# Two edits in a two-block sequence kernel: the keys' norm stands with the queries' norm, and attention divides by its sums once per query block

## The chip, the cores and the metric

The kernel runs on one core of a Trainium2 chip. The metric is device time in microseconds (us), the median over runs; smaller is better. Engines are named as in the profile: PE is TensorE's matmul, PEld its weight load, DVE is VectorE, ACT is ScalarE, POOL is GpSimd, SP is SyncE. L984 means line 984 of the kernel before. In the changed kernel the code from L805 on stands ten lines lower or so (its L853, L864, L869, L923 and L931 are the L843, L854, L859, L913 and L921 of before); this text uses the numbers of before, and only rows that are quoted from the changed kernel carry its own.

## The reference

Input and output are 1024 tokens of 1024 features. The first block has two layers of convolution beside sparse attention, and only its attention matters here; a second block (gated recurrences and an MLP) follows.

```python
def dsa_attention(c_q, c_kv, k_idx, w_idx, q_norm_g, w_uq, w_qidx, kv_norm_g, w_uv, rel_bias):
    k_top = 256
    cq = rmsnorm(c_q, q_norm_g)                          # [1, 1024, 256]
    q = (cq @ w_uq)                                      # 8 heads of 128
    q_idx = (cq @ w_qidx)                                # 8 index heads of 64
    kv = rmsnorm(c_kv, kv_norm_g)                        # [1, 1024, 128], one for all heads
    ...
    score = einsum("bth,bths->bts", w, relu(q_idx . k_idx))   # causal
    _, sel = top_k(score, k_top)                         # 256 keys of each query
    logits = q . kv[sel] * 128 ** -0.5 + rel_bias
    o = softmax(logits) . kv[sel]
    return einsum("bshc,hcd->bshd", o, w_uv)             # 8 heads of 64

x = x + gate * rmsnorm(concat(y_conv, y_attn * silu(g_attn)) @ w_out)
```

## The kernel before

Products in full precision are made of three matmuls of split operands (hi and lo, `mm3`, L269 to L271; the splits are L264 on ACT and L265 on DVE). Activations of a layer lie transposed, features on partitions and the 1024 tokens in two halves of 512 columns. SBUF is cut into pages of 1024 words.

A layer goes through these stages, each of them a generator that yields after a unit of work:

- **Conv inputs**, then **latents** (`g_latents`): keys' latent `kv`, index keys, queries' latent `cq` and its norm. The norm of a half is: Square on ACT (L796), sum over partitions by matmuls with ones (L302), Ln and Exp on ACT (L294, L297, inverse square root), a multiplication on DVE (L801), a split. Ln and Exp need function tables (L288 loads the one that has both).
- **Index scores** (`g_scores`): blocks of 128 queries; c=0 are blocks 2 to 4, c=1 blocks 5 to 7. For each pair of index heads PE makes the heads' queries (copied by L843 on ACT, L844 on DVE) and the products with the index keys (L852); ACT copies these out of PSUM (L854), DVE adds them up (L857, L859).
- **Top-k** (`g_topk`): the 256th largest score of each query is found bit by bit, 31 bits. top1 has blocks 2 to 4: block 2 is counted on DVE (L921), blocks 3 and 4 on ACT (L913), and POOL makes the next threshold from ACT's count (L916, L917, L919). top2 has blocks 5 and 6 on DVE and 7 on ACT.
- **Keys**: `norm_keys` (L984) normalises `kv` by the same steps as the queries (its multiplication is L994), `split_keys` (L998) makes the keys' hi and lo and, by 8 matmuls (L1010), the heads' values.
- **Queries** of all heads, **attention** (`g_attn`, L1095): blocks 0 to 4 while top2 is still counting, then blocks 5 to 7 with the masks of top2. Then the output projection.

Work that fills gaps runs beside these: the convolution (`g_conv`, whose taps are the L703 on DVE) and the gates (`g_gates`, L269 to L271 and L689).

The order on each engine is fixed before the program starts, by a scheduler that works from the order in which the code emits instructions; each engine then runs its own instructions strictly in that order. `weave` interleaves generators in proportion to the units named for each, and `bg=[(generator, rate)]` advances a generator by that many steps for each such unit:

```python
weave((pr(g_latents(), 9), 6), bg=[(conv, RATES[l][1])])     # L1023, RATES[l][1] = 2.0
...
weave((pr(g_scores(wq, 0), 4), 24), (part(gates, g1), g1), bg=[(conv, RATES[l][2])])
weave((pr(g_scores(wq, 1), 4), 24), (part(gates, g2), g2), bg=[(top1, RATES[l][3]), (conv, RATES[l][10])])
norm_keys()
keys = split_keys()
weave((gates, g3_), (top1, 37), bg=[(conv, RATES[l][10]), (top2, RATES[l][5])])
```

In attention a pair of heads has its logits (L1116 to L1124), maximum (L1130 with a mask, L1134 to L1137 without), Exp with the row sum (L1138), and then 1 / sum (L1141), which two matmuls with the identity spread over 64 rows for each head (L1145), the gate's product with it (L1147), transposes (L1154, L1160), values (L1164), and the product of values and gate (L1168).

## Time and profile before

| | |
|---|---|
| median of 3 runs | 3030.16 us (3029.22 to 3030.83) |
| span of the profiled execution | 3029.3 us |
| its own time | within the three runs above, the span is 0.9 us below their median |
| PE | 2906.8 us busy, 96% of the span |
| DVE | 2229.9 us, 74% |
| ACT | 1679.8 us, 55% |
| POOL | 247.2 us, 8% |
| chain that ended last | PE 58%, DVE 5%, POOL 2%, ACT 2%, DMA 1% |
| L913 on ACT | 186 counts, 166.8 us busy, 36.1 us idle until POOL's L919 |

The whole span is PE at 96%, but the two stretches from the first index scores to the end of top2 are not: there DVE and ACT are as full as PE, and POOL, which does nothing elsewhere, is busy. These stretches (196 to 507 us in layer 0, 891 to 1187 us in layer 1) hold nearly everything that the change touches. In the rows below a duration followed by [x <-E t Ln] means that the engine sat idle for x us before it and that instruction Ln of engine E ended that.

### The profile page before, as it was taken

To read this page: it belongs to the slowest core of one execution; us is meant where nothing else is said; L and a number is where in the kernel's file an instruction comes from. 1 tells how busy PE (TensorE), PEld (TensorE's weight loads), DVE (VectorE), ACT (ScalarE), POOL (GpSimd) and SP (SyncE) were. 2 spreads that over 40 slices of the span, in tenths; PEclk is the share of its full clock that TensorE was granted. 3 is DMA by queue.
4 is the path that set the end of the run, shared out by engine and by line. 5 is a ranking of instruction groups with operands and counts; after the bars stand their busy time and mean duration, and the time that the engine had idled before them with its cause. 6 is when DMAs were issued, how large, how long until landed. Compare 5 with 4: busy or idle time off the path is not lost.

```text
span 3029.3 us, 40735 instructions
## 1 busy us (share of the span) xinstructions
PE 2906.8 (96%) x15235; PEld 2362.8 (78%) x15235; DVE 2229.9 (74%) x4118; ACT 1679.8 (55%) x3032; POOL 247.2 (8%) x630
## 2 busy tenths in 40 slices
PE   9998787999999888999999999999999999999999
PEld 6877565778877665777888888888888888888887
DVE  5998899776988899756555667656666587776875
ACT  6248766737147866646444466555555654454454
POOL 0005511000005511000000000000000000000000
PEclk9999989999999989999999999999999999999999
DMA  8222102154101200133122211101013344456443
GB/s 276 63 40 63 42 18 77 48 193 149 39 18 42 63 19 18 36 112 118 49 62 62 79 35 36 56 29 56 29 37 122 103 143 153 151 201 238 153 146 111
DMA packets 218637, 264.14 MB, mean 87 GB/s; under 512 B 11504, under 2 KB 153543, under 8 KB 218439
## 3 DMA queue, kind: packets, MB, share of 16 engines
q1 hardware_dynamic: 218438, 261.54, 26.7%
q8 instruction: 119, 1.95, 0.3%
q14 instruction: 80, 0.65, 0.1%
HBM read 201.21 MB, written 60.29 MB: 86 GB/s over the span
## 4 chain that ended last, share of the span: by engine, by line
PE 58%; DVE 5%; POOL 2%; ACT 2%; DMA 1%; issue 1%; POOLq 0%; ACTq 0%
PE ps L269 15%; PE ps L271 15%; PE ps L270 15%; PE ps L331 5%; PE ps L1499 2%; DVE pg L921 2%; POOL consts L917 1%; PE ps L1164 1%; PE ps L1154 1%; POOL consts L919 1%; POOL consts L916 1%; DMA pg<-in_w_in_dram 1%; PE ps L1488 0%; DVE pg L1130 0%; PE ps L498 0%
## 5 line engine op out<-in xcount | busy, mean ns | idle before, releaser
L269 PE MATMUL ps<-pg,pg 128*128 128x512 f32 (+2 forms) x3080 | 1178.7, 384 | 15.1 <-DVE pg L265 4.2
L270 PE MATMUL ps<-pg,pg 128*128 128x512 f32 (+2 forms) x3080 | 1176.3, 383 | 0.0
L271 PE MATMUL ps<-pg,pg 128*128 128x512 f32 (+2 forms) x3080 | 1176.0, 382 | 0.0
L264 ACT ACTIVATE pg<-pg 128x512 fp32r<-128x512 f32 (+2 forms) x884 | 481.7, 591 | 527.7 <-PE ps L271 157.2
L269 PEld LDWEIGHTS ps<-pg,pg 128*128 128x128 f32 x3080 | 580.5, 189 | 132.9 <-DVE pg L265 10.1
L271 PEld LDWEIGHTS ps<-pg,pg 128*128 128x128 f32 x3080 | 580.6, 189 | 109.8 <-issue 3.7
L270 PEld LDWEIGHTS ps<-pg,pg 128*128 128x128 f32 x3080 | 580.8, 189 | 107.9 <-issue 3.5
L265 DVE TENSOR_TENSOR pg<-pg,pg 128x512 fp32r<-128x512 f32 (+2 forms) x884 | 528.2, 636 | 136.4 <-ACT pg L264 121.3
L278 POOL TENSOR_TENSOR consts<-consts 128x1 f32<-128x1 f32 x56 | 31.3, 559 | 2069.0 <-DVE consts L277 2069.0
L913 ACT ACTIVATE pg<-pg,consts 128x512 bf16<-128x512 uint16 (+5 forms) x186 | 166.8, 897 | 40.8 <-POOL consts L919 36.1
L703 DVE SCALAR_TENSOR_TENSOR pg<-pg,consts,pg 128x512 f32<-128x512 f32 (+15 forms) x256 | 176.9, 742 | 0.4
L331 PE MATMUL ps<-pg,pg 128*128 128x512 f32 x768 | 175.9, 389 | 0.0
L921 DVE TENSOR_SCALAR_CACHE_REDUCE pg<-pg,consts 128x384 bf16<-128x384 uint16 (+5 forms) x186 | 170.9, 919 | 2.3
L331 PEld LDWEIGHTS ps<-pg,pg 128*128 128x128 f32 x768 | 143.8, 188 | 29.6
L1138 ACT ACTIVATE pg<-pg,consts 128x256 f32<-128x256 f32 (+7 forms) x128 | 98.9, 774 | 70.2 <-DVE consts L1130 51.7
L1154 PE MATMUL ps<-consts,pg 128*128 128x128 f32 x576 | 107.7, 291 | 1.9 <-ACT pg L1160 1.1
L852 PE MATMUL ps<-pg,pg 128*128 128x512 f32 (+3 forms) x320 | 86.3, 370 | 14.7 <-DVE pg L844 9.4
L1164 PE MATMUL ps<-pg,pg 128*64 128x128 f32 x1152 | 92.5, 292 | 5.8 <-DVE pg L1147 1.7
L1116 PE MATMUL ps<-pg,pg 128*128 128x384 f32 (+5 forms) x192 | 79.4, 415 | 16.2 <-DVE consts L1130 7.9
L1160 ACT ACTIVATE pg<-ps 128x512 f32<-128x512 f32 (+1 forms) x112 | 57.8, 532 | 66.8 <-PE ps L1154 62.4
L917 POOL TENSOR_SCALAR consts<-consts 128x1 f32<-128x1 f32 x186 | 78.0, 419 | 179.1 <-ACT pg L913 173.5
L1164 PEld LDWEIGHTS ps<-pg,pg 128*64 128x64 f32 x1152 | 64.1, 141 | 35.1 <-issue 13.4
(350 smaller groups left out, 3810.7 us busy)
## 6 DMA issues: line engine op xcount, KB each, us to landing
pg<-in_w_in_dram SPq DMA_DIRECT2D x104, 512.0 KB
pg<-hidden SPq DMA_DIRECT2D x56, 512.0 KB
hidden<-pg SPq DMA_DIRECT2D x48, 512.0 KB
pg<-in_w_ada_dram SPq DMA_DIRECT2D x32, 512.0 KB
pg<-in_w_up_dram SPq DMA_DIRECT2D x32, 512.0 KB
pg<-in_w_down_dram SPq DMA_DIRECT2D x32, 512.0 KB
pg<-in_w_out_dram SPq DMA_DIRECT2D x24, 512.0 KB
x<-pg SPq DMA_DIRECT2D x24, 512.0 KB
```

Source lines behind the costliest of these rows:

```text
L264: self.nc.scalar.activation(hi, src, AF.Copy)
L265: self.nc.vector.tensor_sub(lo, src, hi.bitcast(F32))
L269: nc.tensor.matmul(ps, lhsT=wl, rhs=rh, start=first, stop=False)
L270: nc.tensor.matmul(ps, lhsT=wh, rhs=rl, start=False, stop=False)
L271: nc.tensor.matmul(ps, lhsT=wh, rhs=rh, start=False, stop=last)
L331: nc.tensor.matmul(ps, lhsT=w[z][k], rhs=act[y][k][:, a:b], start=k + n == 0, stop=3 * k + n == 3 * kt - 1)
L703: nc.vector.scalar_tensor_tensor(out, x[:, :512 - d], w, prev[:, d:], op0=OP.mult, op1=OP.add)
L913: nc.scalar.activation(junk_a(b), keys[b], AF.Sign, scale=-1.0, bias=col(tk["half"], b), accum_out=col(tk["cnt"], b))
L917: nc.gpsimd.tensor_scalar(col(tk["tm"], b), col(tk["cnt"], b), lim, -step, op0=OP.is_gt, op1=OP.mult)
L921: nc.vector.tensor_scalar(junk_d(b), keys[b], col(tk["cand"], b), None, op0=OP.is_ge, op1=OP.add, accum_out=col(tk["cnt"], b))
L1154: nc.tensor.transpose(pt[:, c:c + 128], Ps[hi][:, j * 128:j * 128 + 128], self.ident)
L1164: nc.tensor.matmul(uv[hi * 64:hi * 64 + 64], lhsT=V[j // 2][:, v:v + 64], rhs=th[:, jj * 256 + hi * 128:jj * 256 + hi * 128 + 128], start= ...
```

## The change

- `norm_keys` is gone. Its steps stand at the end of `g_latents`, behind the queries' norm, on the same scratch page and function table, in the rotation of PSUM banks 4 to 7 instead of bank 3. `g_latents` has so a seventh unit, and the weave count goes from 6 to 7, so that `conv` (rate 2.0) is advanced by two more steps there.
- In `g_attn` the sums of all eight heads of a query block go to one tile of 8 columns. With the last pair of heads there is one reciprocal of 128x8, eight matmuls that spread it (as many as before in all), one product of the gate of 128x512 and, at the end of the block, one product of values and gate of 128x512. The values of the four pairs lie side by side in PSUM bank 6.
- Two tiles of 8 columns take the place of four of 2; comments and docstrings are gone.

```diff
@@ g_latents
                     self.split(cqh[j][:, s], cql[j][:, s], cq[j][:, s])
                 yield
+            for s in halves:
+                sq = t[:, s]
+                nc.scalar.activation(sq, kv[:, s], AF.Square)
+                ps = self.bank("t", s4)
+                self.sum_rows(ps, [sq])
+                self.bcast_rstd(sq, ps, 128, tab)
+                nc.vector.scalar_tensor_tensor(kv[:, s], kv[:, s], self.vec[f"kv_norm_g{l}"][:, 0:1], sq, op0=OP.mult,
+                                               op1=OP.mult)
+            yield
             self.free(t, cq)
-        def norm_keys():
-            kv = lat["kv"]
-            t = self.page()
-            tab = self.ln_table()
-            for s in halves:
...
-        weave((pr(g_latents(), 9), 6), bg=[(conv, RATES[l][1])])
+        weave((pr(g_latents(), 9), 7), bg=[(conv, RATES[l][1])])
-        norm_keys()
@@ g_attn
+                sm = self.ring("sums", self.sums)
+                uvs = self.bank("pu", [6])
                 for hp in range(4):
...
-                    nc.vector.reciprocal(sm, sm)
-                    pu = self.bank("pu", [6])
-                    uv, rb = pu[:, :128], pu[:, 128:256]
-                    for hi in range(2):
-                        nc.tensor.matmul(rb[hi * 64:hi * 64 + 64], lhsT=sm[:, hi:hi + 1].to_broadcast([128, 64]),
-                                         rhs=self.ident, start=True, stop=True)
-                    nc.vector.tensor_mul(gb[:, hp], gb[:, hp], rb)
+                    uv = uvs[:, hp * 128:hp * 128 + 128]
+                    if hp == 3:
+                        nc.vector.reciprocal(sm, sm)
+                        rb = self.bank("pt", [4, 5])
+                        for h in range(8):
+                            nc.tensor.matmul(rb[h % 2 * 64:h % 2 * 64 + 64, h // 2 * 128:h // 2 * 128 + 128],
+                                             lhsT=sm[:, h:h + 1].to_broadcast([128, 64]), rhs=self.ident, start=True,
+                                             stop=True)
+                        nc.vector.tensor_mul(gb, gb, rb)
...
-                    nc.vector.tensor_mul(yb[:, hp], uv, gb[:, hp])
+                nc.vector.tensor_mul(yb, uvs, gb)
```

The change of emission moves instructions on every engine. Three places follow; a row is the line, the operation, what is written, what is read, and the size.

**PE in layer 0, in the stage of the keys.** Before, the sum of the keys' squares (L302, from page 23) stands in the midst of the gates' matmuls, which come from page 21 and 19 ahead of it and from page 39 and 35 behind it.

```order
L270 MATMUL ps_62<-pg7_57_303,pg21_163_2416 128x512
L271 MATMUL ps_62<-pg48_49_295,pg21_163_2416 128x512
L302 MATMUL ps_62<-pg23_171_2643,consts_58 128x512
L269 MATMUL ps_62<-pg41_42_288,pg39_168_2534 128x512
L270 MATMUL ps_62<-pg49_50_296,pg35_167_2533 128x512
```

In the changed kernel the same gate matmuls are followed by the values' (its L1006, the L1010 of before), which read the normalised keys.

```order
L269 MATMUL ps_62<-pg48_49_295,pg19_164_2439 128x512
L270 MATMUL ps_62<-pg7_57_303,pg35_163_2438 128x512
L271 MATMUL ps_62<-pg48_49_295,pg35_163_2438 128x512
L1006 MATMUL ps_62<-pg24_178_2660,pg38_104_974 128x512 x4
```

What moved: the sums of the keys' squares left this place; nothing between the scores and the values waits for Ln of the keys.

**DVE in layer 0, where c=0 of the scores goes over into c=1 and top1 begins.** Before, the first preparations of top1 (L902 to L904, L940) and the scores of c=1 (L857, L859) come ahead of the first count (L921); the first tap (L703) behind them is row 325.

```order
L940 TENSOR_SCALAR pg17_148_1689<-pg36_133_1343,consts_58 128x512
L904 TENSOR_SCALAR pg17_148_1689<-pg36_133_1343,consts_58 128x512
L857 TENSOR_SCALAR pg12_140_1667<-pg27_143_1670,consts_58 128x1024
L844 TENSOR_TENSOR pg15_145_1672<-ps_62,pg15_145_1672 64x384 x2
L857 TENSOR_SCALAR pg0_141_1668<-pg9_144_1671,consts_58 128x896
L904 TENSOR_SCALAR pg26_147_1688<-pg16_132_1342,consts_58 128x640
L904 TENSOR_SCALAR pg26_147_1688<-pg16_132_1342,consts_58 128x384
L859 SCALAR_TENSOR_TENSOR pg0_141_1668<-pg27_143_1670,consts_58,pg0_141_1668 128x896
L921 TENSOR_SCALAR pg28_146_1687,consts_58<-pg26_147_1688,consts_58 128x384
```

In the changed kernel 45 taps of one channel (page 12, rows 303 to 333) stand there with a single other instruction among them, the queries of the second pair of index heads of c=1 (row 315, its L854, after 12 taps). The last rows of that block of taps, and what follows:

```order
L703 SCALAR_TENSOR_TENSOR pg12_140_1624<-pg29_92_818,consts_58,pg12_140_1624 128x500 x2
L703 SCALAR_TENSOR_TENSOR pg12_140_1624<-pg29_92_818,consts_58,pg12_140_1624 128x499 x2
L703 SCALAR_TENSOR_TENSOR pg12_140_1624<-pg29_92_818,consts_58,pg12_140_1624 128x498 x2
L867 TENSOR_SCALAR pg27_143_1692<-pg9_144_1693,consts_58 128x768
L869 SCALAR_TENSOR_TENSOR pg27_143_1692<-pg15_145_1694,consts_58,pg27_143_1692 128x768
L905 TENSOR_SCALAR consts_58<-consts_58 128x1
L911 TENSOR_SCALAR consts_58<-consts_58 128x1
L905 TENSOR_SCALAR consts_58<-consts_58 128x1 x2
L908 TENSOR_SCALAR consts_58<-consts_58 128x3
```

What moved: a whole channel's taps, which before are strewn over top1, stand in one piece ahead of the second product of c=1 and ahead of all of top1. Counted over the stage: of taps there are 20 before the first L921 and 47 in top1 before, and 68 and 2 in the changed kernel. Page 15, which the row L869 reads, is the one that ACT's next copy out of PSUM writes. In layer 1 no such block is formed (2 and 46 taps before; 20 and 29 now, one or a few at a time). L921 of top2 between the end of top1 and the first row of attention: 10 before and 1 now in layer 0, 9 and 4 in layer 1; those are made in attention, ahead of top2's end, 52 before and 61 now, 53 and 58.

**ACT in layer 1, ahead of the scores.** Before, between the second L796 (squares of the queries) and the first copy for the scores:

```order
L689 ACT_TABLE_LOAD
L689 ACTIVATE pg_493_6850<-ps 128x512
L294 ACT_TABLE_LOAD
L294 ACTIVATE pg_485_6772<-ps,consts 128x512
L297 ACT_TABLE_LOAD
L297 ACTIVATE pg_485_6772<-pg_485_6772 128x512
L264 ACTIVATE pg_481_6768<-pg_473_6618 128x512
L264 ACTIVATE pg_482_6769<-pg_474_6619 128x512
L726 ACTIVATE pg_495_7144<-pg_487_6809 128x15
L689 ACT_TABLE_LOAD
L689 ACTIVATE pg_493_6850<-ps 128x512
L843 ACTIVATE pg_492_6837<-ps 128x384
```

In the changed kernel the keys' steps (its L808, L294, L297) lie in the same place, and the table changes between them; the rows from the queries' Exp to the first copy:

```order
L297 ACT_TABLE_LOAD
L297 ACTIVATE pg_484_6698<-pg_484_6698 128x512
L294 ACT_TABLE_LOAD
L294 ACTIVATE pg_484_6698<-ps,consts 128x512
L297 ACT_TABLE_LOAD
L297 ACTIVATE pg_484_6698<-pg_484_6698 128x512
L264 ACTIVATE pg_480_6694<-pg_472_6544 128x512
L264 ACTIVATE pg_481_6695<-pg_473_6545 128x512
L808 ACTIVATE pg_484_6698<-pg_460_6397 128x512
L689 ACT_TABLE_LOAD
L689 ACTIVATE pg_492_6798<-ps 128x512
L853 ACTIVATE pg_491_6785<-ps 128x384
```

What moved: ahead of the copy stand two more table loads, an Ln, an Exp and two squares; two more loads with the second Ln and Exp stand right behind it. In layer 0 the same place has one load less ahead of the copy (the queries' second Exp follows its Ln directly) and two more behind it.

## Rows read from the trace of the kernel before

**Rows 1.** The profile's page, its first part: busy time of each engine, with share of the span and instructions.

```profile
PE 2906.8 (96%) x15235; PEld 2362.8 (78%) x15235; DVE 2229.9 (74%) x4118; ACT 1679.8 (55%) x3032; POOL 247.2 (8%) x630
```

**Rows 2.** Busy time by stage (windows). Columns: stretch, its length, busy us and instructions of each engine, granted TensorE clock, DMA share, GB/s. The first four are layer 0: from the first L844 to the first count that keeps going, to the end of top1 (the L934 that closes its last bit), to the first L1134 of attention, to the last L921 of top2; the next four are the same marks in layer 1; the last two are attention's blocks 5 to 7.

```profile
196.00:247.10 51.10, 48.75 (x236) 40.49 (x235) 39.60 (x69) 26.86 (x53) 3.10 (x8) 1.00 0.42 83
247.10:354.30 107.20, 87.95 (x360) 67.96 (x358) 92.83 (x221) 87.94 (x181) 80.79 (x184) 0.92 0.17 52
354.30:396.40 42.10, 32.52 (x122) 22.08 (x120) 41.20 (x91) 36.86 (x64) 7.71 (x32) 0.96 0.08 26
396.40:506.60 110.20, 94.95 (x673) 71.25 (x674) 104.92 (x336) 70.81 (x165) 15.40 (x62) 0.86 0.16 48
891.20:931.80 40.60, 40.38 (x194) 32.83 (x193) 27.84 (x49) 24.98 (x47) 2.50 (x5) 1.00 0.16 46
931.80:1039.20 107.40, 91.47 (x387) 71.63 (x386) 93.16 (x222) 88.74 (x187) 82.55 (x187) 0.95 0.17 52
1039.20:1079.80 40.60, 35.83 (x140) 25.93 (x138) 39.84 (x88) 35.03 (x61) 7.15 (x28) 0.95 0.18 53
1079.80:1187.40 107.60, 92.25 (x655) 68.33 (x653) 102.74 (x337) 69.79 (x164) 14.98 (x60) 0.89 0.05 16
...
545.00:636.00 91.00, 87.28 (x651) 66.10 (x652) 66.39 (x124) 61.70 (x96) 0.00 (x0) 0.98 0.33 108
1226.00:1306.00 80.00, 79.19 (x605) 58.36 (x606) 56.73 (x112) 56.40 (x90) 0.00 (x0) 1.00 0.23 71
```

**Rows 3.** PE's timeline at the keys' norm, layer 0 and layer 1. Columns: start us, us, engine, line, operation, operands, idle before and its releaser.

```profile
346.24 2.07 PE L302 MATMUL ps<-pg,consts 128*128 128x512 f32 x2 [12.62 <-ACT pg L294]
...
1029.79 2.08 PE L302 MATMUL ps<-pg,consts 128*128 128x512 f32 x2 [8.27 <-ACT pg L294]
```

**Rows 4.** DVE's timeline at the same two places.

```profile
347.45 0.75 DVE L994 SCALAR_TENSOR_TENSOR pg<-pg,consts,pg 128x512 f32<-128x512 f32 x1 [7.28 <-ACT pg L297]
...
1031.11 0.75 DVE L994 SCALAR_TENSOR_TENSOR pg<-pg,consts,pg 128x512 f32<-128x512 f32 x1 [4.04 <-ACT pg L297]
```

**Rows 5.** DVE's instructions by line, from 396.4 to 506.6 us (attention's first part in layer 0). Columns: busy us, mean ns of one, idle before them.

```profile
L921 DVE TENSOR_SCALAR_CACHE_REDUCE pg<-pg,consts 128x768 bf16<-128x768 uint16 (+3 forms) x52 | 55.9, 1075 | 0.8
...
L1168 DVE TENSOR_TENSOR pg<-ps,pg 128x128 f32<-128x128 f32 x20 | 5.7, 287 | 0.9 <-PE ps L1164 0.9
L1147 DVE TENSOR_TENSOR pg<-pg,ps 128x128 f32<-128x128 f32 x20 | 5.7, 285 | 1.4 <-PE ps L1145 1.0
...
L1141 DVE RECIPROCAL consts<-consts 128x2 f32<-128x2 f32 x20 | 3.2, 159 | 0.0
```

**Rows 6.** The product of PSUM and a page of 128x512 on DVE (one line, all its instructions; ns min, median, max), and the matmuls that spread 1 / sum (by line, whole span).

```profile
L1087 DVE TENSOR_TENSOR pg<-ps,pg x16: 684/692/692, 605.6 to 1318.5; 128x512 f32<-128x512 f32 x16
...
L1145 PE MATMUL ps<-consts 128*64 128x128 f32 x256 | 30.4, 319 | 21.0 <-DVE consts L1141 17.2 <-DVE pg L1168 2.6 <-DVE consts L931 1.1
```

**Rows 7.** DVE's timeline in layer 0: a run of taps ahead of the scores and what follows it, then the passage from c=0 to c=1.

```profile
184.72 3.52 DVE L703 SCALAR_TENSOR_TENSOR pg<-pg,consts,pg 128x512 f32<-128x512 f32 x5
188.15 0.54 DVE L449 TENSOR_SCALAR pg<-ps 8x384 f32<-8x384 f32 x1
...
241.76 0.56 DVE L844 TENSOR_TENSOR pg<-ps,pg 64x384 fp32r<-64x384 f32 x1 [4.57 <-ACT pg L843]
245.08 0.56 DVE L844 TENSOR_TENSOR pg<-ps,pg 64x384 fp32r<-64x384 f32 x1 [2.76 <-ACT pg L843]
...
249.41 1.00 DVE L859 SCALAR_TENSOR_TENSOR pg<-pg,consts,pg 128x768 f32<-128x768 f32 x1
```

**Rows 8.** ACT's timeline in top1 of layer 0: counts with taps on DVE (to 336.8 us), then without.

```profile
333.25 0.72 ACT L913 ACTIVATE pg<-pg,consts 128x512 bf16<-128x512 uint16 x1 [0.87 <-POOL consts L919]
...
336.80 0.72 ACT L913 ACTIVATE pg<-pg,consts 128x512 bf16<-128x512 uint16 x1 [1.44 <-POOL consts L919]
...
338.73 0.72 ACT L913 ACTIVATE pg<-pg,consts 128x512 bf16<-128x512 uint16 x1
```

**Rows 9.** POOL's timeline beside them: the same instruction with taps on DVE and without.

```profile
335.18 1.31 POOL L917 TENSOR_SCALAR consts<-consts 128x1 f32<-128x1 f32 x1
...
337.05 0.30 POOL L917 TENSOR_SCALAR consts<-consts 128x1 f32<-128x1 f32 x1
```

**Rows 10.** ACT by line and shape in top1 of layer 0 (247.1 to 354.3 us). Columns as in rows 5.

```profile
L913 ACT ACTIVATE pg<-pg,consts 128x640 bf16<-128x640 uint16 x16 | 13.2, 827 | 6.1 <-POOL consts L919 5.8
...
L913 ACT ACTIVATE pg<-pg,consts 128x512 bf16<-128x512 uint16 x16 | 11.5, 721 | 7.4 <-POOL consts L919 6.7 <-DVE consts L952 0.5
...
L294 ACT ACTIVATE pg<-ps,consts 128x512 f32<-128x512 f32 x2 | 1.4, 678 | 0.1
L288 ACT ACT_TABLE_LOAD x1 | 1.3, 1283 | 0.0
L297 ACT ACTIVATE pg<-pg 128x512 f32<-128x512 f32 x2 | 1.2, 619 | 0.0
```

**Rows 11.** ACT's timeline ahead of the scores of layer 1.

```profile
882.49 1.28 ACT L294 ACT_TABLE_LOAD   x1 [0.31 <-PE ps L302]
883.79 0.69 ACT L294 ACTIVATE pg<-ps,consts 128x512 f32<-128x512 f32 x1
884.50 1.28 ACT L297 ACT_TABLE_LOAD   x1
885.79 0.63 ACT L297 ACTIVATE pg<-pg 128x512 f32<-128x512 f32 x1
```

More of the change, by code (lines that the diff above doesn't have):

```diff
@@ L37 @@
 NPAGES = 50
-CWORDS = 1500
+CWORDS = 1516
 NOWN = 4
@@ L432, in rest @@
             self.mx = [self.const(2) for _ in range(4)]
-            self.sums = [self.const(2) for _ in range(4)]
+            self.sums = [self.const(8) for _ in range(2)]
             self.x1 = [self.tc.dram_tile([T, D], F32, name=f"x{i}") for i in range(2)]
@@ L981, in g_topk @@
             self.free(cnt_pg, kps, late=True)
-        def norm_keys():
-            kv = lat["kv"]
-            t = self.page()
-            tab = self.ln_table()
-            for s in halves:
-                sq = t[:, s]
-                nc.scalar.activation(sq, kv[:, s], AF.Square)
-                ps = self.bank("k", [3])
-                self.sum_rows(ps, [sq])
-                self.bcast_rstd(sq, ps, 128, tab)
-                nc.vector.scalar_tensor_tensor(kv[:, s], kv[:, s], self.vec[f"kv_norm_g{l}"][:, 0:1], sq, op0=OP.mult,
-                                               op1=OP.mult)
-            self.free(t)
         def split_keys():
@@ L1100, in g_attn @@
                 near = min(256, n)
-                gb = cut(GP[:, b % 2 * 512:b % 2 * 512 + 512], 4, 128)
-                self.dma(gb, self.gate[0:512, q].rearrange("(h p) t -> p h t", p=128))
+                gb = GP[:, b % 2 * 512:b % 2 * 512 + 512]
+                self.dma(cut(gb, 4, 128), self.gate[0:512, q].rearrange("(h p) t -> p h t", p=128))
                 if b % 2 == 0:
                     YA.append(self.page())
-                yb = cut(YA[b // 2][:, b % 2 * 512:b % 2 * 512 + 512], 4, 128)
+                yb = YA[b // 2][:, b % 2 * 512:b % 2 * 512 + 512]
+                sm = self.ring("sums", self.sums)
+                uvs = self.bank("pu", [6])
                 for hp in range(4):
@@ L1108, in g_attn @@
                     mx = self.ring("mx", self.mx)
-                    sm = self.ring("sums", self.sums)
                     for h in (2 * hp, 2 * hp + 1):
@@ L1127, in g_attn @@
                         Ps.append(pg)
-                        m1, s1 = mx[:, h % 2:h % 2 + 1], sm[:, h % 2:h % 2 + 1]
+                        m1, s1 = mx[:, h % 2:h % 2 + 1], sm[:, h:h + 1]
                         if b >= 2:
@@ L1167, in g_attn @@
                     self.free(Ps)
-                    nc.vector.tensor_mul(yb[:, hp], uv, gb[:, hp])
+                    if hp == 3:
+                        nc.vector.tensor_mul(yb, uvs, gb)
                     yield
```

## The prediction

> **What bounds the kernel now.** The page first: PE is busy for 96% of the span [rows 1], so a gain must shorten PE's waits, and these lie where PE is not the bound. The windows by stage show where that is: from the first index scores to the end of top2 a layer takes 310.6 us (51.1 + 107.2 + 42.1 + 110.2) in layer 0 and 296.2 us in layer 1; DVE is busy for 278.5 and 263.6 of it, PE for 264.2 and 259.9 [rows 2]. Three parts of these have different limits. In top1 ACT and POOL hand each bit to each other, with DVE 87% busy. From the end of top1 to attention DVE is full: 41.2 of 42.1 us, 39.8 of 40.6. From there to the end of top2 it is full too: 104.9 of 110.2, 102.7 of 107.6 [rows 2]. After that, with top2 gone, PE is the bound: 87.3 of 91.0 and 79.2 of 80.0 us in blocks 5 to 7 [rows 2]. So I ask of every edit when top1 ends, and how much DVE work stands between that and the last count of top2; what follows is shifted by the same amount.
>
> **The keys' norm.** Before, PE waits 12.6 us in layer 0 and 8.3 us in layer 1 for the Ln of the keys [rows 3], and DVE 7.3 and 4.0 us for their Exp [rows 4]. Gone, but PE's 20.9 us are no gain of their own: at the time top1 is still counting, and top2 and attention wait for that. What top1 itself gains is ACT's work in it: one table load 1.3, two Ln 1.4, two Exp 1.2, so 3.9 us [rows 10], and what DVE's wait held up.
>
> Where it goes, it costs. In layer 1 two loads, an Ln, an Exp and two squares (taken as an Exp) come ahead of the first copy for the scores: 2 x 1.28 + 0.69 + 3 x 0.63 = 5.1 us [rows 11], and the second Ln and Exp delay what is behind it. Nothing else hides it, since the queries of the scores are what PE needs next; the two more steps of the convolution put also seven more matmuls there. I take 6 us later. In layer 0 the load that is saved pays for the squares, and only the second Ln and Exp with two loads lie behind the copy, 3.9 us, part of which PE's queue covers: 2 us (0 to 4).
>
> The price of a load is the one figure on which the pages and the rows differ. The rows show 1.28 us, and the next instruction starting 0.01 us behind it: 882.49 + 1.28 is 883.77, the Ln starts at 883.79 [rows 11]. The Trainium skill, in "ScalarE: Activation LUTs", section "What ACT_TABLE_LOAD costs", gives 2.66 us for a switch, a drain of 1.38 us included. By it the four more loads of layer 1 would cost 5.5 us more than by the row; this trace does not agree, and I sum by the row.
>
> **The block of taps in layer 0.** The same two steps reach further than their seat. In layer 0 the taps of a whole channel, 45, now stand ahead of top1 in one piece, with the queries of c=1's second pair after 12 of them. DVE runs in order, so the first score after it waits for all of them, and behind that score stand ACT's next copy (its page is the one read), PE's third product and top1's first preparations. Working it out: the gates' 15 more matmuls ahead of these queries cost 3 us at PE's pace of this stretch (48.75 us busy for 236 instructions, 0.21 each [rows 2]), the start 2 us, so L844 comes at 241.8 + 5 = 247 instead of 241.8 [rows 7]. Then 33 taps; five take 188.15 - 184.72 = 3.43 us [rows 7], so 33 take 22.6, to 270 with L844's own 0.56. Two operations of 768 columns (1.00 and about 0.6 [rows 7]), ACT's copy, and the preparations (some ten small ones) bring the first count to 275, against 247.1. PE stands still for some 20 us of this, where before it waited hardly (48.75 of 51.1 [rows 2]), and comes back at the low clock for a few us.
>
> Not all of the 28 us is lost, because the taps leave top1. With taps on DVE a bit of two blocks takes 336.80 - 333.25 = 3.55 us, without 338.73 - 336.80 = 1.93 [rows 8]; between them POOL's L917 falls from 1.31 to 0.30 us [rows 9]. ACT's work in top1 was 87.9 us busy in 107.2 [rows 2], of the 19 us of waiting 12.5 for POOL [rows 10]. Now its keys' norm (3.9) goes, while copies of gates and values and the first counts of top2 join, about 9 us by their 0.6 to 0.9 each: 93 us busy, and with 2 taps for 47 I let 3 us of waiting stand. Top1 takes 96 us (88, if neighbours overlap everywhere, to 103) and ends at 371, 17 later than 354.3.
>
> Then DVE's work: the 42.1 us to attention lose 9 L921 at 1.08 (9.7), four splits at about 0.69 (the nearest size [rows 6]) and a dozen small operations at 0.16 [rows 5], so some 15: 27 us, attention begins at 398 instead of 396.4. But these nine counts (with their small ones 11 us) and four operations of the convolution of 128x512 with one of the bias table of twice that (0.69 for 512 [rows 6], so 3.7 with their overlap) now lie in front of top2's end: 110.2 + 14.7 - 3.5 (next part) = 121.4, so top2 ends at 519.5, 13 later. The 3.7 us are missing behind it and come back there. **Layer 0: +9** (0 to +14).
>
> **Layer 1** has no such block: taps ahead of the first L921 rise from 2 to 20, into time in which DVE was idle (27.8 of 40.6 busy [rows 2]), and in top1 they fall from 46 to 29. In layer 0 top1 waited 19 us with 47 taps in it, 0.4 us a tap: 17 make 7. With the 3.9 of the keys' norm and part of DVE's 4.0, top1 takes 98 instead of 107.4 and ends at 1039.2 + 6 - 9.4, 3 earlier. To attention five L921 and some small ones less (7), to the end of top2 five more (6, less 3 of the next part): **layer 1: -7** (-13 to +1).
>
> **Once per block.** Before, a pair costs DVE 0.159 + 0.285 + 0.287 us [rows 5]; four pairs 2.92. Now a reciprocal of eight columns (about 0.16, as small ones are) and two products of 128x512 at 0.69, the row nearest in shape [rows 6], 1.54. Instructions here overlap by about 0.08 each, so twelve against three save 0.7 us less: 0.7 us a block (0 to 1.4), 3.5 for the five blocks in DVE's full stretch; it is in both sums. In blocks 5 to 7 DVE has slack (66.4 of 91 [rows 2]): nothing. PE's waits for the reciprocal, 17.2 us in both layers [rows 6], fall from four a block to one, but lie where DVE sets the end, so they are worth no more than DVE's 3.5. The eight matmuls are the same number. The last product holds the only bank of values until the block's end; the next block's logits, some us of PE work, stand between: nothing, or 0.3 us a block if not.
>
> Sum: 9 - 7 = +2 on the profiled execution's 3029.3, which stands 0.9 below the median: **3032 us** (3030.2 + 2).
>
> **The rivals.** A measurement of this kernel can tell about 0.2%, 6.06 us, from no change: the bounds are 3024.1 and 3036.2.
> (a) Forecast, block and gains cancel: 3032, own range 3025 to 3036, 0.40.
> (b) Faster: the block costs layer 0 nothing, because DVE makes up its order (its sum of work there is the same, 278 us, and the taps go into 11.5 us idle before 247 [rows 2]); this needs ACT to run top1 at its 88 us, ending at 363: layer 0 then +1, and layer 1 at -13 if its top1 does likewise: 3018. Decides from a top1 of under 92 us in both layers. For it: the 1.93 us of a bit without taps; against: ACT also serves the scores. 0.25.
> (c) Slower: ACT keeps its waits, not for POOL but for PE, which, 20 us late, has 60 us of scores and gates to catch up; top1 of layer 0 then lasts 104 us, +17, and layer 1 gains nothing in top1 beyond the norm, -1: 3046. Decides from 100 us on. 0.30.
> (d) A load costs more than its row shows, by a drain: layer 1 is later by 5.5, layer 0 by 1.4: 3039; 0.05 (this is the rule of "ScalarE: Activation LUTs" above, with which the trace does not agree).
>
> **How the numbers follow.** (b) is faster, (a) the same, (c) and (d) slower: 0.25, 0.40, 0.35. The range goes from just below (b)'s 3018, with 1 in 10 left out below, to (c)'s 3046, with as much above: 3016 to 3047.
>
> **What would show it.** In the changed kernel: no wait of PE's at the keys' norm; in layer 0 one wait of some 20 us in PE's timeline near 252 us, the first steady L913 near 275, end of top1 near 371, attention near 398, last L921 near 519; in layer 1 the first copy for the scores 5 to 6 us later, top1 of 98 us; L917 near 0.3 us in top1 of layer 0; three operations instead of twelve in a block at 0.69. Wrong would make it: taps that are quicker next to an idle POOL, a top1 below 92 us, or a scheduler's gap in layer 1 that I have not seen in its order.

## The result, and the profile after

The changed kernel is slower by half a per cent: a median of 3045.9 us (3042.1 to 3050.0) against 3030.0 us (3029.2 to 3030.8) for the kernel before on the same chip, a ratio of 1.0053 [1.0038, 1.0067]. The profiled execution spans 3043.7 us, against 3029.3.

The first part of the page, which answers to [rows 1]:

```profile
PE 2896.3 (95%) x15235; PEld 2368.0 (78%) x15235; DVE 2225.3 (73%) x3974; ACT 1674.9 (55%) x3034; POOL 222.9 (7%) x630
```

PE does the same 15235 matmuls in 10.5 us less busy time and the span is 14.4 us longer: PE is idle for about 25 us more. The windows by stage (the first four layer 0, the last four layer 1) show where. The marks are those of [rows 2], but that the first stretch of each layer starts here at ACT's copy, 0.5 us ahead of the first L854 (the L844 of before):

```profile
193.40:272.00 78.60, 52.27 (x252) 43.55 (x250) 74.50 (x120) 31.98 (x59) 3.13 (x5) 0.88 0.28 50
272.00:374.80 102.80, 96.30 (x392) 76.33 (x393) 73.17 (x189) 90.91 (x195) 62.59 (x188) 0.94 0.20 65
374.80:400.60 25.80, 21.70 (x85) 16.23 (x84) 23.52 (x49) 22.11 (x41) 10.01 (x27) 0.92 0.07 21
400.60:519.50 118.90, 93.68 (x684) 71.43 (x683) 116.19 (x323) 74.66 (x172) 18.03 (x65) 0.89 0.16 49
905.90:952.50 46.60, 45.40 (x217) 37.29 (x216) 40.66 (x69) 31.31 (x56) 2.98 (x5) 1.00 0.13 40
952.50:1053.30 100.80, 92.90 (x393) 72.94 (x393) 82.58 (x204) 89.28 (x191) 72.25 (x187) 0.98 0.19 60
1053.30:1085.70 32.40, 26.74 (x107) 19.95 (x105) 31.51 (x69) 20.69 (x39) 4.32 (x16) 0.95 0.15 45
1085.70:1194.80 109.10, 86.69 (x633) 67.91 (x633) 105.25 (x306) 75.59 (x172) 17.63 (x76) 0.88 0.05 15
```

In layer 0 the first stage, taken from L844 in both, has 78.1 us instead of 51.1, and PE idles for 26.3 of it. Top1 is 4.4 us shorter, the way to attention 16.3 shorter, the way to the end of top2 8.7 longer. From one layer's latents (the first L773) to the next's, layer 0 takes 706.6 us instead of 696.7. Layer 1, up to the last product of its convolution branch (L1087), behind which its output projection begins, takes 474.1 instead of 472.8. What follows, this projection and the second block, which the change doesn't touch, takes 1713.2 instead of 1710.1; over all fourteen profiles of this study it takes 1709.2 to 1714.4, so 3 us of it say nothing, and in what follows I compare the layers.

The long wait is at the place which the order showed. DVE's timeline in layer 0, where the taps stand in one piece (L854 of after is L844 of before, L869 is L859):

```profile
243.69 0.56 DVE L854 TENSOR_TENSOR pg<-ps,pg 64x384 fp32r<-64x384 f32 x1
244.28 2.28 DVE L703 SCALAR_TENSOR_TENSOR pg<-pg,consts 128x499 f32<-128x499 f32 x3
246.60 19.88 DVE L703 SCALAR_TENSOR_TENSOR pg<-pg,consts,pg 128x512 f32<-128x512 f32 x30
266.39 0.62 DVE L867 TENSOR_SCALAR pg<-pg,consts 128x768 f32<-128x768 f32 x1
267.05 1.02 DVE L869 SCALAR_TENSOR_TENSOR pg<-pg,consts,pg 128x768 f32<-128x768 f32 x1
```

ACT's and then PE's timeline beside it:

```profile
268.16 1.02 ACT L864 ACTIVATE pg<-ps 128x1024 f32<-128x1024 f32 x1 [19.82 <-DVE consts L905]
...
271.99 0.72 ACT L923 ACTIVATE pg<-pg,consts 128x512 bf16<-128x512 int16 x1
```

```profile
246.19 2.11 PE L862 MATMUL ps<-pg,pg 128*128 128x512 f32 x8
271.90 1.86 PE L862 MATMUL ps<-pg,pg 128*128 128x448 f32 x4 [23.60 <-ACT pg L864]
```

They are read together: 33 taps hold DVE for 22.2 us (244.28 to 266.48), the score's addition L869 comes behind them, ACT's next copy L864 waits for it, since its page is the one that L869 reads (the row names L905, the next small instruction behind L869), and PE's next product waits for the copy. So PE stands still for 23.6 us. What was to go is gone too: of PE's waits for a norm's sums 0.5 us is left in the whole span, against the 20.9 us of [rows 3].

### The profile page after: what moved, and what is told of

Read it like the earlier page. It is cut to its first block, busy times and chain, and to the rows that moved or that the text cites. A ratio compares the mean times of both kernels' runs of the same rounds, so it can differ in the third digit from the quotient of the medians.

```text
span 3043.7 us, 40552 instructions
## 1 busy us (share of the span) xinstructions
PE 2896.3 (95%) x15235; PEld 2368.0 (78%) x15235; DVE 2225.3 (73%) x3974; ACT 1674.9 (55%) x3034; POOL 222.9 (7%) x630
## 4 chain that ended last, share of the span: by engine, by line
PE 71%; DVE 17%; ACT 5%; issue 2%; DMA 2%; POOL 2%; SPq 0%; POOLq 0%; ACTq 0%; DVEq 0%
PE ps L269 18%; PE ps L270 18%; PE ps L271 18%; DVE pg L931 5%; PE ps L331 5%; DVE pg L703 3%; PE ps L1498 2%; PE ps L1152 1%; PE ps L1162 1%; ACT pg L923 1%; DVE pg L1126 1%; DMA pg<-in_w_in_dram 1%; DVE pg L869 1%; DVE pg L265 1%; POOL consts L927 1%
## 5 line engine op out<-in xcount | busy, mean ns | idle before, releaser
L269 PEld LDWEIGHTS ps<-pg,pg 128*128 128x128 f32 x3080 | 581.5, 189 | 136.3 <-DVE pg L265 9.9
L270 PEld LDWEIGHTS ps<-pg,pg 128*128 128x128 f32 x3080 | 582.3, 189 | 110.5 <-DVE pg L265 3.5
L271 PEld LDWEIGHTS ps<-pg,pg 128*128 128x128 f32 x3080 | 581.7, 189 | 108.4 <-issue 3.3
L265 DVE TENSOR_TENSOR pg<-pg,pg 128x512 fp32r<-128x512 f32 (+2 forms) x884 | 528.1, 635 | 161.0 <-ACT pg L264 145.8
L923 ACT ACTIVATE pg<-pg,consts 128x512 bf16<-128x512 uint16 (+5 forms) x186 | 166.4, 895 | 21.9 <-POOL consts L929 17.8
L703 DVE SCALAR_TENSOR_TENSOR pg<-pg,consts,pg 128x512 f32<-128x512 f32 (+15 forms) x256 | 174.5, 740 | 1.0 <-PE ps L271 0.5
L331 PEld LDWEIGHTS ps<-pg,pg 128*128 128x128 f32 x768 | 143.8, 188 | 29.6
L1134 ACT ACTIVATE pg<-pg,consts 128x256 f32<-128x256 f32 (+7 forms) x128 | 98.8, 772 | 70.4 <-DVE consts L1126 54.4
L1152 PE MATMUL ps<-consts,pg 128*128 128x128 f32 x576 | 103.8, 292 | 9.4 <-ACT pg L1134 5.1
L1112 PE MATMUL ps<-pg,pg 128*128 128x384 f32 (+5 forms) x192 | 78.1, 408 | 29.1 <-DVE consts L1126 19.2
L862 PEld LDWEIGHTS ps<-pg,pg 128*128 128x128 f32 x320 | 58.6, 197 | 59.2 <-ACT pg L864 37.0
L864 ACT ACTIVATE pg<-ps 128x384 f32<-128x384 f32 (+5 forms) x96 | 71.3, 754 | 48.5 <-DVE consts L905 19.8
L1152 PEld LDWEIGHTS ps<-consts,pg 128*128 128x128 f32 x576 | 67.7, 144 | 35.2 <-issue 18.0
```

The source lines that it names most:

```text
L265: self.nc.vector.tensor_sub(lo, src, hi.bitcast(F32))
L269: nc.tensor.matmul(ps, lhsT=wl, rhs=rh, start=first, stop=False)
L270: nc.tensor.matmul(ps, lhsT=wh, rhs=rl, start=False, stop=False)
L271: nc.tensor.matmul(ps, lhsT=wh, rhs=rh, start=False, stop=last)
L331: nc.tensor.matmul(ps, lhsT=w[z][k], rhs=act[y][k][:, a:b], start=k + n == 0, stop=3 * k + n == 3 * kt - 1)
L703: nc.vector.scalar_tensor_tensor(out, x[:, :512 - d], w, prev[:, d:], op0=OP.mult, op1=OP.add)
```

## The experiments

Layer times are of the profiled execution: layer 0 from its latents to those of layer 1, layer 1 from there to the last product of its convolution branch, ahead of its output projection. All ratios are to the kernel before.

| run | ratio [95%] | layer 0, us | layer 1, us |
|---|---|---|---|
| before | 1 | 696.7 | 472.8 |
| after | 1.0053 [1.0038, 1.0067] | 706.6 | 474.1 |
| e1_taps_only | 1.0102 [1.0087, 1.0117] | 717.9 | 483.0 |
| e2_norm_no_advance | 1.0017 [1.0008, 1.0025] | 693.7 | 476.2 |
| e3_attn_only | 0.9993 [0.9984, 1.0001] | 692.2 | 471.4 |
| e4_norm_only | 1.0057 [1.0045, 1.0070] | 709.0 | 475.7 |
| e5_one_table | 0.9992 [0.9984, 1.0001] | 691.6 | 471.3 |
| e6_block_only_undone | 1.0006 [0.9997, 1.0015] | 694.6 | 475.7 |
| e7_norm_mid | 1.0007 [0.9998, 1.0016] | 697.2 | 471.8 |
| e8_one_table_l1adv | 1.0000 [0.9992, 1.0009] | 692.5 | 474.2 |
| e9_one_step | 1.0031 [1.0020, 1.0043] | 702.7 | 473.1 |
| e10_four_steps | 1.0060 [1.0046, 1.0074] | 711.3 | 472.1 |
| e11_one_table_four | 1.0031 [1.0020, 1.0041] | 706.1 | 468.3 |
| e12_twice_per_block | 0.9989 [0.9980, 0.9998] | 692.1 | 472.4 |

After, e6, e9 and e10 have the same code in layer 1, and it takes 472.1 to 475.7 us: a layer of one profile is good to about 2 us.

### Is it the block of taps?

**e1_taps_only**: the kernel before, with nothing but two more steps of the convolution in that weave.

```diff
-RATES = ((1.0, 2.0, 0.2, ...), (1.0, 2.0, 0.2, ...))
+RATES = ((1.0, 2.29, 0.2, ...), (1.0, 2.29, 0.2, ...))
```

> The kernel before with one number changed: the convolution's rate beside the latents is 2.29 instead of 2.0, so that it is advanced by two more steps there, as in the changed kernel; the norm and attention are untouched. The fixed order then has 12 and 32 taps in a row at the passage from c=0 to c=1 of layer 0, as the changed kernel has 12 and 33. Theory T (the block of taps makes the loss): PE waits 20 us or more there, top1 begins near 270 us, and the whole is 10 to 18 us slower than before: 3040 to 3048. Rival N (the loss is made by the norm's new place, by table loads and work ahead of the scores): nothing of that is in here, 3028 to 3033.

The block forms (12 taps, the queries' addition, 32 taps), with the wait that it makes in PE's timeline (here the lines of before):

```profile
269.61 1.86 PE L852 MATMUL ps<-pg,pg 128*128 128x448 f32 x4 [21.40 <-ACT pg L854]
```

It costs more than expected, 21 us in layer 0 and 10 in layer 1. In layer 0 the first steady count comes 22.9 us late and the end of top2 still 22.3: without the move of the norm nothing is given back. In layer 1, where the order has no such block, the first steady count comes 3.8 us late, and the way from the end of top1 to attention takes 6.6 us more, with 14 of DVE's top2 counts in it instead of 9; why the order puts them there stays open.

**e2_norm_no_advance** and **e6_block_only_undone**: the changed kernel without the two steps, in both layers, and in layer 0 alone.

```diff
# e2, in g_latents and at its weave
-            yield
-        weave((pr(g_latents(), 9), 7), bg=[(conv, RATES[l][1])])
+        weave((pr(g_latents(), 9), 6), bg=[(conv, RATES[l][1])])
# e6
+        weave((pr(g_latents(), 9), 6), bg=[(conv, (2.0, 2.29)[l])])
```

> The changed kernel without the seventh unit (no yield behind the keys' norm, count 6), so that the convolution is not advanced: norm and attention as changed, the order has no block of taps, and 47 and 46 taps in top1 as before. Theory T: layer 0 loses its 13 us and more, layer 1 its late passage of about 5: 3022 to 3030. Rival N: the table loads and the late scores are all still there, 3038 to 3046.

> The changed kernel with the convolution advanced as before in layer 0 and as changed in layer 1: the order of layer 0 has no block of taps, layer 1 has 29 taps in top1 as in the changed kernel. Theory T: layer 0 ends 13 us earlier than in the changed kernel, layer 1 takes as long: 3031 to 3035. Rival: the block is made up for later (e2 gained by layer 1's order): 3038 to 3046.

Without the block layer 0 takes 693.7 and 694.6 us, 12 to 13 less than in the changed kernel, and e6's ratio is 1.0006 against 1.0053. So the block makes some 13 of the 16 us, and without it in layer 0 (e6) there is no difference from before that can be told. But the gain that e2 was to leave did not come either: at 1.0017 [1.0008, 1.0025] it is a little slower than before. In layer 0 it starts attention 13.2 us earlier than before, yet ends top2 only 1.6 earlier, because counts moved behind that mark; in layer 1 it loses 3.4 us.

PE's waits in e2 show why the keys' stall was worth so little. It is replaced (columns: waiting line, releaser, sum in us, times, longest; L1005 is the values' matmul, L1010 of before):

```profile
PE ps L1005 <- ACT pg L1006: 13.1, 4, 9.1
```

Ahead of top1's end PE waited 12.6 and 8.3 us for the Ln [rows 3]; in e2 it waits 13.1 us over four places for the copies of the keys' values, which stand behind top1's counts on ACT. (In the changed kernel, where the block makes PE late anyway, these waits are 1.5 us.)

**e9_one_step**: e6 with one step instead of none in layer 0. **e10_four_steps**: with four, with which the order has no run of ten taps, but taps strewn among block 2's counts.

```diff
-        weave((pr(g_latents(), 9), 6), bg=[(conv, (2.0, 2.29)[l])])
+        weave((pr(g_latents(), 9), 6), bg=[(conv, (2.1479, 2.29)[l])])     # e9
+        weave((pr(g_latents(), 9), 6), bg=[(conv, (2.5764, 2.29)[l])])     # e10
```

> e6 with the convolution advanced by one step in layer 0 (e6: none, the changed kernel: two); layer 1 as in the changed kernel. Its order forms the block again: 14 and 32 taps in a row ahead of top1. Theory T (the block itself is the loss, whatever made it): as the changed kernel, 12 to 14 us above e6, 3043 to 3047. Rival A (the loss grows with the advance): half of it, 3037 to 3041.

> The same with four steps in layer 0: by its order no run of ten or more taps stands at the passage, and 43 taps are in top1. Theory T: no loss, as e6, 3029 to 3034. Rival A: twice the loss of the changed kernel, 3055 or more.

One step is enough for the block (32 taps) and for a wait of PE of 21.4 us; layer 0 is 6 us over before instead of 10. That is 8 us above e6, where theory T had 12 to 14, and the median, 3041.3, stands just above rival A's range. Yet the passage is as late as in the changed kernel (first steady count at 271.7 us against 271.9); what is shorter is top1 behind it, 98.2 us against 102.8, and the way from there to attention, 23.2 against 25.8. So the block sets how late top1 starts; how much of that is lost hangs on what follows as well. Four steps were to show that it is the run without a break that hurts. They showed the opposite of what I expected; PE's and DVE's timeline in e10:

```profile
285.81 0.80 PE L269 MATMUL ps<-pg,pg 128*128 128x512 f32 x1 [32.69 <-DVE pg L265]
```

```profile
253.41 3.39 DVE L703 SCALAR_TENSOR_TENSOR pg<-pg,consts,pg 128x512 f32<-128x512 f32 x5
...
258.16 0.61 DVE L930 TENSOR_SCALAR_CACHE_REDUCE pg<-pg,consts 128x384 bf16<-128x384 int16 x1
```

Taps and counts (L930 here) take turns, and behind all of them on DVE stands the split of the next gate weights (L265), for which PE waits 32.7 us. So the length of a run of taps is not the measure. By these traces it is how much DVE work of any kind stands ahead of the instruction that PE needs next; layer 0 takes 711.3 us, 4.7 more than with the block in one piece, and the median, 3049.5, lies between T and A.

### What each half of the change is worth

**e3_attn_only**: the kernel before with the attention part of the change alone. **e4_norm_only**: the changed kernel with the attention of before.

```diff
# e3 (e4 is its reverse in the changed kernel)
+                    uv = uvs[:, hp * 128:hp * 128 + 128]
+                    if hp == 3:
+                        nc.vector.reciprocal(sm, sm)
...
+                        nc.vector.tensor_mul(gb, gb, rb)
...
-                    nc.vector.tensor_mul(yb[:, hp], uv, gb[:, hp])
+                    if hp == 3:
+                        nc.vector.tensor_mul(yb, uvs, gb)
```

> The kernel before with attention's part of the change alone (one reciprocal, one spread, one product and one last product per query block). Theory T: DVE saves 3.5 us in each layer's full stretch, 3023 to 3027. Rival W (in the changed kernel's trace PE waits 6.8 us for one single reciprocal at the end of layer 1's top2, 13.5 us in all, with ACT's last count of top2 queued behind it): the eight sums' one reciprocal is late where a pair's was early, no gain, 3029 to 3036.

> The changed kernel with attention as before: norm, seventh unit and block of taps alone. Theory T: the loss stays and attention's 7 us of gain are missing, 3049 to 3053. Rival W: attention's part costs rather than gains, so without it the kernel is quicker than the changed one, 3036 to 3044.

Attention's part alone gives -0.07%, with an interval that touches no change, and e4, which lacks it, stands a microsecond over after, where theory T had put 3 to 7 and rival W a gain. The profile shows a gain of 4.5 us in layer 0 and 1.4 in layer 1 in e3, and also what stops it. DVE's and ACT's timeline in e3 at the end of layer 0's top2 (lines as in before):

```profile
495.16 1.14 DVE L921 TENSOR_SCALAR_CACHE_REDUCE pg<-pg,consts 128x896 bf16<-128x896 uint16 x1
...
506.70 0.15 DVE L934 TENSOR_SCALAR consts<-consts 128x1 f32<-128x1 f32 x1 [1.43 <-POOL consts L919]
```

```profile
504.76 1.15 ACT L913 ACTIVATE pg<-pg,consts 128x1024 bf16<-128x1024 uint16 x1 [1.12 <-POOL consts L919]
```

DVE's last count comes 10 us earlier than in before, but top2's last step waits for ACT's last count of block 7, which is where it was. Not all of the 10 us is saved work: four operations of 1.28 us (L466) that stood ahead of this count in before stand behind it here. With DVE relieved, ACT and POOL are the end of top2, which closes at 506.7 us instead of 507.4; most of the 4.5 us is gained behind it.

### Where the keys' norm could stand

**e5_one_table**: the norm in the queries' loop on a page of its own, both Ln under one table and both Exp behind them, no seventh unit.

```diff
-            t = self.page()
+            t, tk = self.pages(2)
...
+                ks = tk[:, s]
+                nc.scalar.activation(ks, kv[:, s], AF.Square)
...
+                nq = nc.scalar.activation(sq[0], ps, AF.Ln, ...)
+                nk = nc.scalar.activation(ks, pk, AF.Ln, ...)
+                nc.scalar.activation(sq[0], sq[0], AF.Exp, scale=-0.5)
+                nc.scalar.activation(ks, ks, AF.Exp, scale=-0.5)
```

> As e2 (norm and attention as changed, convolution not advanced), but the keys' norm lies inside the loop of the queries' norm: squares of both, Ln of both, Exp of both for a half, on a second scratch page. By its order there are 2 table loads ahead of the scores in each layer instead of 5 before and 10 in the changed kernel's layer 1. Theory S (what e2 loses to before is the scores' late start in layer 1, 5 us by the traces, made by the loads and the steps between them): the start comes 1 to 2 us earlier than before instead of 5 later, the whole is 5 to 8 us below e2: 3026 to 3029. Rival D (DVE's work to the end of top2 sets the time, the start does not): as e2, 3032 to 3036.

It tests the price of the start. ACT's timeline ahead of layer 1's scores, after and then e5, to the first copy for the scores (L853, in e5 L855):

```profile
896.85 1.28 ACT L294 ACT_TABLE_LOAD   x1
898.15 0.69 ACT L294 ACTIVATE pg<-ps,consts 128x512 f32<-128x512 f32 x1
898.85 1.28 ACT L297 ACT_TABLE_LOAD   x1
...
902.35 1.28 ACT L689 ACT_TABLE_LOAD   x1
...
905.87 0.49 ACT L853 ACTIVATE pg<-ps 128x384 fp32r<-128x384 f32 x1 [1.63 <-PE ps L271]
906.38 1.28 ACT L294 ACT_TABLE_LOAD   x1
```

```profile
880.78 0.69 ACT L803 ACTIVATE pg<-ps,consts 128x512 f32<-128x512 f32 x1 [2.13 <-PE ps L302]
881.50 0.63 ACT L807 ACTIVATE pg<-pg 128x512 f32<-128x512 f32 x1
882.16 1.28 ACT L689 ACT_TABLE_LOAD   x1
...
886.90 0.49 ACT L855 ACTIVATE pg<-ps 128x384 fp32r<-128x384 f32 x1 [1.81 <-PE ps L271]
```

From the start of the layer to this copy after takes 49.5 us, e2 49.4, before and e5 44.3. One way through Ln and Exp instead of two gives back the whole 5 us that e2 had lost at the start, though not the 1 to 2 us more that I had expected (ahead of the copy stand 2 loads in e5, 5 in before, and 7 of the changed kernel's 10). The two layers of e5 take 7.0 us less than those of e2, with the same edits otherwise. Against before it gains nothing that can be told (0.9992).

**e7_norm_mid**: e3 with `norm_keys()` called between c=0 and c=1 of the scores, so that the stall lies elsewhere. **e8_one_table_l1adv** and **e11_one_table_four**: e5 with two more steps in layer 1, and with four in layer 0.

```diff
# e7: after the weave of g_scores(wq, 0)
+        norm_keys()
# e8: RATES[1][1] 2.0 -> 2.29; e11:
+        weave((pr(g_latents(), 9), 6), bg=[(conv, (2.5764, 2.0)[l])])
```

> e3 (attention's part alone) with the keys' norm called between c=0 and c=1 of the scores instead of behind c=1. Nothing of it stands ahead of the scores, and PE's matmuls of the keys' stage do not wait for its Ln. Theory D (DVE and ACT set the end of top1 and top2, PE's 21 us of waiting lie beside them): 3024 to 3030, as e3. Rival P (PE's wait is a loss of its own): 10 us or more below e3, 3010 to 3018.

> e5 with the convolution advanced by two steps in layer 1 alone, where the order strews the taps (25 in top1 instead of 46) and forms no block. If top1 gains from fewer taps, as the changed kernel's layer 1 did (100 us for 107): 2 to 4 us below e5. If not, as e5 or above.

> e5 (one function table for both norms) with four steps of advance in layer 0 and none in layer 1, as a candidate below both kernels: 42 taps in top1 of layer 0 instead of 47, 46 in layer 1. At 0.4 us a tap 2 us below e5, 3023 to 3027; if ACT and DVE are bound by other work there, as e5.

e7 gains nothing over e3; its layer 0 takes 5 us more. Again the values' copies take the wait (14.6 us in all, 9.8 the longest). That nothing is gained by taking away the 21 us of [rows 3] is so shown twice, by e2 and e7; in both, 13 to 15 us of them come back at the values. e8 takes 2.9 us more in layer 1 than e5, at the edge of the scatter, and no less in the median: more taps early are no gain there. Its top1 is shorter, as hoped (103.0 us for 108.2), but the way from the first copy for the scores to the first steady count is longer by 7.5 us. These are the windows of that way in e5 and in e8 (columns as in [rows 2]):

```profile
886.90:926.60 39.70, 39.61 (x192) 32.72 (x191) 30.24 (x52) 25.17 (x49) 2.45 (x5) 1.00 0.16 47
```

```profile
886.70:933.90 47.20, 47.20 (x226) 38.86 (x225) 45.14 (x77) 27.08 (x51) 2.94 (x5) 1.00 0.15 45
```

PE is busy for the whole of both, and the two steps put 34 more matmuls into it. e11 missed for e10's reason: PE waits 32.6 us for L265, and layer 0 takes 14.5 us more than in e5.

**e12_twice_per_block**: e5 with reciprocal, spread and gate product for four heads at a time.

```diff
-                    if hp == 3:
-                        nc.vector.reciprocal(sm, sm)
+                    if hp % 2 == 1:
+                        h0 = 2 * hp - 2
+                        nc.vector.reciprocal(sm[:, h0:h0 + 4], sm[:, h0:h0 + 4])
```

> e5 with attention's reciprocal, spread and product made twice per query block, for the first four heads and for the last four (the last product of values and gate stays one). DVE has two operations more a block (about 0.4 us). Theory W (a part of what once per block saves is given back, because PE's matmuls wait for one reciprocal that stands late on a full DVE, 11.5 us in e5's trace): that wait falls below 8 us and the whole by 1 to 4 us: 3023 to 3026. Rival (the wait lies beside DVE's and ACT's counts of top2): as e5 or 1 to 3 us above, 3027 to 3030.

It is the one version whose interval lies below before, 0.9989 [0.9980, 0.9998], 3.3 us, but that is hardly told from e5: PE's waits for the reciprocal sum to 13.6 us in it against 11.5, where theory W had them below 8, and only the longest is shorter (5.0 against 7.5).

## Why the prediction was right or wrong

The time came out inside the range that was given, but the likeliest case, 3032 and no difference that can be told, is not what came: 3045.9, slower. It is about the number of rival (c), and by part of its mechanism only. That the number fits is luck: (c) had +17 and -1 for the layers, which made +9.9 and +1.3, and 4.7 us of the median lie outside them.

**Layer 0, right in size and steps.** Forecast +9, measured +9.9. PE's wait 23.6 us (some 20); first steady count at 272 to 273.7 (275); attention at 400.6 (398); last count of top2 at 519.5 (519.5); then 3.0 us come back (3.7). e1, e2 and e6 show the cause, and e10 corrects its wording: not "one piece", but what is queued ahead on DVE. That the same late start cost e9 4 us less says that the size, +9, hung on top1 and what follows it as well.

One term in it was off, and the total hid that. Top1 was to take 96 us and took 102.8, because I let 3 us of waiting stand on ACT, which was idle for 11.9 (102.80 less 90.91). Its waits there by releaser (columns: waiting line, releaser, sum in us, times, longest):

```profile
ACT pg L864 <- PE ps L862: 6.7, 5, 3.5
ACT pg L923 <- POOL consts L929: 2.6, 3, 1.6
```

POOL's share fell as forecast, from 12.5 us [rows 10]. In its place came waiting for PE, which was late with the scores: rival (c)'s mechanism, at 6.7 us. Top1 was over the 100 us from which (c) was to decide, yet (c)'s +17 for the layer did not follow, since less of DVE's work was left behind top1: attention began only 4.2 us later than before.

**Layer 1, wrong by 8 us.** Forecast -7, measured +1.3, with 2 us of uncertainty; the four profiles with this code give -0.7 to +2.9. Two steps held: the first copy for the scores 5.2 us later (6), and POOL's waits in top1 down from 16.6 to 8.8 us, 7.8 (7 for 17 taps). Three terms were mis-sized, by 12.2 us together:
- Top1 gained 6.6 us, not 9.4, so 2.8 less. ACT is as busy in it as before (89.28 us, 88.74 in [rows 2]): the 3.9 us of the keys' norm went, and copies and counts moved into their seat.
- The way from the first copy to the first steady count takes 46.5 us instead of 41.0. I had put the seven moved matmuls into the 6 us ahead of the copy and held the 18 more taps to be free, since DVE had idle time. PE is busy there for 45.4 of 46.6 us: with 21 more matmuls in this stretch (217 instead of 196, counted from the copy in both) it, and not DVE, set the time. This cost 5.5 us where I had put none. The two steps make it: without them the way takes 41.9 us (e2), with them 46.9 (e6), and e8 against e5 shows the same.
- What follows the last count of top2. I had put nothing there. The last bit closes 6.75 us behind DVE's last count (4.2 in before), and by the end of the layer another 1.4 us are lost: 3.9 in all.

Against these 12.2 us stand 3.5 that came out better: 0.8 at the start, 8.2 us less from top1 to attention (7), and 1.5 us more from there to the last count (3). That leaves 8.7, from the -7.4 that the terms add up to before rounding to the measured +1.3.

The rows behind the third, in PE's, DVE's and ACT's timeline of the changed kernel (its L1139 is the reciprocal, L1142 the matmuls that spread it, L1152 the transposes, L1158 ACT's copies of them, L944 closes the last bit):

```profile
1195.43 1.98 PE L1142 MATMUL ps<-consts 128*64 128x128 f32 x16 [6.84 <-DVE consts L1139]
```

```profile
1195.18 0.20 DVE L1139 RECIPROCAL consts<-consts 128x8 f32<-128x8 f32 x1
...
1201.55 0.15 DVE L944 TENSOR_SCALAR consts<-consts 128x1 f32<-128x1 f32 x1 [0.97 <-POOL consts L929]
```

```profile
1198.28 0.60 ACT L1158 ACTIVATE pg<-ps 128x512 f32<-128x512 f32 x1 [7.68 <-PE ps L1152]
1199.12 0.60 ACT L1158 ACTIVATE pg<-ps 128x512 f32<-128x512 f32 x1 [0.24 <-PE ps L1152]
1199.61 1.14 ACT L923 ACTIVATE pg<-pg,consts 128x1024 bf16<-128x1024 uint16 x1
```

The one reciprocal of the block stands on DVE behind top2's counts. PE waits for it 6.8 us, ACT's copies of the transposes (L1158) wait for PE 7.7 us, and behind them on ACT stands block 7's last count (L923), and so top2's end. I had written that PE's waits for the reciprocal lie where DVE sets the end. They do, but ACT's count stands behind them in the queue. The rows show this chain, and not that the one reciprocal makes the 3.9 us: in e4, where each pair has its own, PE waits 1.8 us and ACT's copies 2.4 us at the same place, and the last bit closes 6.5 us behind DVE's last count all the same. From the start of the layer top2 closes after 345.2 us, in before after 345.1. How much of this term is the reciprocal's stays open.

**Once per block, right in durations, too high in worth.** The estimates 0.16, 0.69 and 0.69 us were 0.196, 0.686 and 0.684. These are DVE's times in the changed kernel, all instructions of a line, min/median/max in ns:

```profile
L1139 DVE RECIPROCAL consts<-consts x16: 190/196/204, 420.0 to 1298.2; 128x8 f32<-128x8 f32 x16
...
L1145 DVE TENSOR_TENSOR pg<-pg,ps x16: 677/686/689, 421.9 to 1305.2; 128x512 f32<-128x512 f32 x16
...
L1167 DVE TENSOR_TENSOR pg<-ps,pg x16: 680/684/691, 423.1 to 1314.9; 128x512 f32<-128x512 f32 x16
```

The 7 us in both sums were DVE's saving. e3 shows what reached the end, about 2 us in the median and 4.5 + 1.4 in the profile, because the end of top2 passes to ACT.

**The table load, right.** In the rows above the Ln starts 0.01 us behind the end of the load before it (896.85 + 1.28 = 898.13, then 898.15), as in [rows 11]. Rival (d) did not come: it asked for 5.5 us more at the start of layer 1, and the start was 5.2 late where the rows asked for 6. The Trainium skill's 2.66 us for a switch ("ScalarE: Activation LUTs", section "What ACT_TABLE_LOAD costs") is not what this trace shows.

**What stays open.** After's median is 15.9 us above before's, its two layers account for 11.2 and what follows them for 3.1 in the profile. Whether that last is the change's or the scatter of this part between executions, the profiles can't tell. Nor do the runs show why top1 behind the block takes 102.8 us in the changed kernel and 98.2 in e9.

## What to carry to other kernels

Where each engine runs its queue strictly in order, an edit that only shifts background work must be read from the new order: find the next instruction that a bound engine needs, and add up all that now stands ahead of it on the engine that makes it, whether in one run or mixed. A long wait on the busiest engine is a gain only if nothing behind it stands on a second full engine; here 21 us of PE's waits were worth nothing (e2, e7): most came back at the values' copies on ACT, and neither version is quicker for it. Merging small steps into one at the end of a block saves time on its engine, but makes whoever needs the result wait for the whole queue, and an unrelated instruction behind the waiter then waits too; here the saving hardly reached the end, and no run shows the merging to be a loss.

## What was unexpected of the hardware

After its long wait PE runs at the lower of its two clocks, as had been allowed for, but for a price that I had not worked out: it is small. The windows around the wait:

```profile
271.90:276.50 4.60, 4.60 (x11) 3.64 (x12) 4.60 (x12) 4.51 (x10) 3.03 (x8) 0.50 0.12 48
276.50:284.00 7.50, 6.76 (x30) 5.32 (x29) 7.09 (x22) 6.57 (x15) 5.36 (x17) 0.96 0.20 76
```

For 4.6 us the granted clock is 0.50, then 0.96. The 11 matmuls of the first stretch take 0.42 us each, the 30 behind them 0.23, so by an estimate from these rows the low clock cost about 2 us (11 times 0.19) on top of a wait of 23.6.

A reciprocal of four times the columns (128x8 for 128x2) takes 0.196 instead of 0.159 us, and a product of four times the columns 0.69 instead of 0.285. If the time grows evenly with the columns, an estimate from these pairs, 0.15 us of each does not depend on them: nearly all of the reciprocal of 128x2, and half of the product of 128x128.
